# Sums of squares in DRAM, x loaded ahead for the last rows, and six places for stationary operands, in a bidirectional hybrid layer

## The chip, the cores and the metric

The kernel runs on one core of a Trainium2 chip. The core has a matrix engine (PE, with its weight loads shown apart as PEld), a vector engine (DVE), a scalar engine (ACT), GpSimd (POOL), and SyncE (SP), whose queue issues nearly all transfers. The engines run side by side; each takes its own instructions in order and waits on semaphores for the others. The metric is the device time of one execution in microseconds (us).

## The reference, cut to what matters

```python
h = rms_norm(x, norm_g) * (1 + scale) + shift          # scale, shift, gate from silu(c) @ w_ada
z = h @ w_in + b_in                                    # 2048 x 2048 times 2048 x 4096
u_pool, u_lru, g_pool, g_lru = four quarters of z
y_pool = pool_mixer(u_pool)                            # windowed means, 256 x 256 product per group
y_lru  = rg_lru(conv4(u_lru))                          # gates by products, a scan each way, summed
y_pool = rms_norm(y_pool, out_norm_pool_g) * silu(g_pool)
y_lru  = rms_norm(y_lru,  out_norm_lru_g)  * silu(g_lru)
y = concat(y_pool, y_lru) @ w_out + b_out              # 2048 x 2048 times 2048 x 2048
out = rms_norm(x + gate * y, final_norm_g)
```

Everything is float32, the sequence has 2048 rows and the model width is 2048. The two middle norms need, for each row, the sum of squares over the 1024 channels of the pooling half and over the 1024 of the recurrent half, that is over four groups of 256 channels each.

## The kernel before, in words

**Steps.** The program is one loop over 368 steps t. A step is 24 matmuls of 128x512: a stationary operand `s` (in pool `s`) against a moving operand `m` (three places, pool `m`). Both are float32 numbers split in two parts, and three of the four products of parts are taken, so a product of 128 channels costs three matmuls. Steps 0 to 255 are the input projection: eight groups of 32 steps (L0, P3, L1, L2, P2, L3, P1, P0; L is a recurrent head, P a pooling group), in each four blocks `tb` of 512 rows with eight steps. Steps 256 to 367 are the output projection, in two halves `sg` of 56 steps; each does seven products instead of eight by sums and differences of quarter matrices (A11, A12, S2, S3, A22, S1, S4), eight steps a product, first for q=0 and then for q=1.

**Lists by step.** `at(t, fn)` puts work into step t, behind its matmuls. `m_load` issues the moving operand four steps ahead, `m_split` (L160: ACT copy L169, DVE subtraction L170) splits it two steps ahead. `unit_load` and `unit_split` (L267, L285) make a stationary operand of the output projection; u counts them, four for a product, and `unit_at` says in which step. SP's queue has loads and stores in one order, and an instruction that waits there holds up those behind it.

**Gated groups.** For each group and block, `merge` (L563, recurrent) or `fin` (L637, pooling) multiplies the result with its gate and stores it to DRAM (`yscr`). It also squares it (L570, L648) and adds the squares to a tile of 128x2048 (L572, L650): `sq["L"]` and `sq["P"]`, each in one of the eight places of pool `big`. The last pooling group has its blocks at steps 240, 246, 250 and 256, the last recurrent head its blocks 3, 2, 1, 0 at 225, 231, 237 and 243.

**Norms.** `rn(tb, kind)` (by `rms_chain`, L391) takes a block's slice: one float32 matmul with a matrix of ones (L393) sums over partitions, then ACT takes the root (L394) and DVE the reciprocal (L395). The eight calls stand at steps 244 to 259. `normed` (L278) multiplies the stored groups with it when they become stationary operands; blocks 0 and 1 are used in the first half, blocks 2 and 3 in the second.

**Rows out.** `out_evac` (L712) gathers the products in row tiles `o` (eight places of `big`). For each row tile and half of its columns `x_load` brings x into a place of pool `raw` (eight places, shared by all loads), `x_add` (L744) adds `b_out` times gate (`gb`), `part_fin` (L748) multiplies with the gate, adds x, and squares on ACT (L755); `out_row` (L763) sums the squares, takes root and reciprocal, scales (L775) and stores. The last four steps (364 to 367) are held back and done tile by tile, with `part_fin` and `out_row` of each tile behind it; the moving operand of step 367 is called `ml`.

**Order.** A list scheduler at build time sets each engine's order. It takes the program's order as priority and lets an instruction pass when another isn't ready by its reckoning. PE, DVE and ACT then run that order whatever is late.

Of the kernel before, what the change touches and what calls it, by code (L numbers as in the profile page):

```python
# [44 lines left out]
def layer(ctx: ExitStack, tc: tile.TileContext, xc, xn, c, wada, win, wgate, wpool, wout, vecs, consts, bout, fng, out):  # L45
    nc = tc.nc
    pool = lambda name, bufs, **kw: ctx.enter_context(tc.tile_pool(name=name, bufs=bufs, **kw))
    one = pool("one", 1)
    s_p = pool("s", 8)
    m_p = pool("m", 3)  # L50
    raw_p = pool("raw", 8)
    big_p = pool("big", 8)

    mix_pools = [tc.alloc_tile_pool(name=n, bufs=b, side="right") for n, b in (("tmp", 9), ("gw", 1), ("uch", 1))]
    tmp_p, gw_p, uch_p = mix_pools
# [41 lines left out]
    def V(name, i, n=1):  # L97
        return vec[:, VO[name] + i:VO[name] + i + n]
# [123 lines left out]
    def c_fin():  # L222
# [3 lines left out]
            nc.tensor.matmul(out=ps[:, n:n + 1], lhsT=a[:, n * 128:(n + 1) * 128], rhs=ones[:, 0:1], start=True, stop=True)  # L226
        vtt(out=bias, in0=ps[:, 0:4], in1=V("b_in", 0, 4), op=ALU.add)

    def w_split(g, p):
        r = wraw.pop((g, p))  # L230
        s = s_p.tile([128, 2, 2, TB], F32R, tag="s", name="s")
# [243 lines left out]
        vtt(out=w[:, 1], in0=r, in1=w.bitcast(F32)[:, 0], op=ALU.subtract)  # L475
        gw["t"] = w

    def sq_alloc(kind):
        t = big("sq" + kind)[:, :S]
        nc.gpsimd.memset(t, 0.0)  # L480
        sq[kind] = t

    def lru_unit(g, h, d, tb, b, last):

# [78 lines left out]
        def merge():  # L563
            hf, gr = st["hf"], st["g"]
            silu(g, gr)
            for i in range(2):
                vtt(out=hf[:, i], in0=hf[:, i], in1=st["t", i], op=ALU.add)
            for i in range(2):
                stt(out=gr[:, i], in0=hf[:, i], scalar=V("gn_lru", 2 * h + i), in1=gr[:, i], op0=ALU.mult, op1=ALU.mult)
                act(out=hf[:, i], in_=hf[:, i], func=AF.Square)  # L570
                v = sq["L"][:, tb * TB:(tb + 1) * TB]
                vtt(out=v, in0=v, in1=hf[:, i], op=ALU.add)  # L572
            store(out=yscr[g][tb], in_=gr)
            if last:
                del u_t[g]

# [13 lines left out]
    def pool_unit(g, q, tb, b, last):  # L590
        w = WINDOWS[q]
        lo = w // 2
        hi = w - lo - 1
        st = {}

        def sums():
            if tb == 0:
                r = raw("pwr")
                load(out=r[:, :, :256], in_=wpool[q])
                pw = raw_p.tile([128, 2, 2, 256], F32R, tag="raw", name="pw")  # L600
                act(out=pw[:, 0], in_=r[:, :, :256], func=AF.Copy)
                vtt(out=pw[:, 1], in0=r[:, :, :256], in1=pw.bitcast(F32)[:, 0], op=ALU.subtract)
                gw["p"] = pw
            U = u_t[g]
            st["x"] = x = uch_p.tile([128, 2, 2, TB], F32R, tag="uch", name="uch")
            for i in range(2):
                t = tmp("pt")
                n = TB + w - 2
                o = PAD + tb * TB - lo
                eng = vtt  # L610
                eng(out=t[:, :n], in0=U[i][:, o:o + n], in1=U[i][:, o + 1:o + 1 + n], op=ALU.add)
                k = 2
                while k < w:
                    n -= k
                    eng(out=t[:, :n], in0=t[:, :n], in1=t[:, k:k + n], op=ALU.add)
                    k *= 2
                t = t[:, :TB]
                if tb == 0:
                    vtt(out=t[:, :lo], in0=t[:, :lo], in1=cst[:, EO[w]:EO[w] + lo], op=ALU.mult)
                if tb == 3 and hi:  # L620
                    vtt(out=t[:, TB - hi:], in0=t[:, TB - hi:], in1=cst[:, EO[w] + lo:EO[w] + lo + hi], op=ALU.mult)
                stt(out=t, in0=t, scalar=1.0 / w, in1=U[i][:, usl(tb)], op0=ALU.mult, op1=ALU.subtract)
                act(out=x[:, 0, i], in_=t, func=AF.Copy)
                vtt(out=x[:, 1, i], in0=t, in1=x.bitcast(F32)[:, 0, i], op=ALU.subtract)
            if last:
                del u_t[g]

        def mix():
            for m in range(2):
                ps = px()  # L630
                for j in range(2):
                    mm3(ps, gw["p"], slice(m * 128, (m + 1) * 128), st["x"], j, j == 0, j == 1)
                st["ps", m] = ps
            st["g"] = raw("gl")
            load(out=st["g"], in_=gscr[g][tb])

        def fin():  # L637
            gr = st["g"]
            for m in range(2):
                c_ = 2 * q + m  # L640
                y = tmp("py")[:, :TB]
                act(out=y, in_=st.pop(("ps", m)), func=AF.Identity, scale=V("pool_scale", c_), bias=pbias[:, c_:c_ + 1])
                st["y", m] = y
            silu(g, gr)
            for m in range(2):
                y = st["y", m]
                stt(out=gr[:, m], in0=y, scalar=V("gn_pool", 2 * q + m), in1=gr[:, m], op0=ALU.mult, op1=ALU.mult)
                act(out=y, in_=y, func=AF.Square)  # L648
                v = sq["P"][:, tb * TB:(tb + 1) * TB]
                vtt(out=v, in0=v, in1=y, op=ALU.add)  # L650
            store(out=yscr[g][tb], in_=gr)

        at(b, sums)
        at(b + 1, mix)
        at(b + 2, fin)
# [29 lines left out]
    def rows_open():  # L685

        for p in reversed(mix_pools):
            p.release()
        row_p = ctx.enter_context(tc.tile_pool(name="row", bufs=1, side="right", reuse_waits="tile"))
        for n in ("gb", "fg", "gate"):  # L690
            fin[n] = row_p.tile([128, D], F32, tag=n, name=n)
        load(out=fin["gb"], in_=bout.broadcast_to([128, D]))
        load(out=fin["fg"], in_=fng.broadcast_to([128, D]))
        fin["rn"] = row_p.tile([128, 4, TB], F32, tag="rn", name="rn")
        for i, (tb, kind) in enumerate([(2, "P"), (2, "L"), (3, "P"), (3, "L")]):
            act(out=fin["rn"][:, i], in_=rn_t[tb, kind], func=AF.Copy)
            rn_t[tb, kind] = fin["rn"][:, i]
        sq.clear()

    def gate_rows(i):  # L700
        t = raw("dg")[:, 0]
# [33 lines left out]
    def row_of(sg, n):  # L735
        return 8 * sg + n

    def x_load(sg, n, h):
        r = raw("x").rearrange("p j t -> p (j t)")
        i = row_of(sg, n)  # L740
        load(out=r, in_=xn[i * 128:(i + 1) * 128, h * 1024:(h + 1) * 1024])
        x_t[sg, n, h] = r
# [5 lines left out]
    def part_fin(sg, n, h, lo, hi, slot):  # L748
# [10 lines left out]
    def half_fin(sg, n, h):  # L759
        x_add(sg, n, h)  # L760
        part_fin(sg, n, h, 0, 1024, h)

    def out_row(sg, n, slots, parts):  # L763
        i = row_of(sg, n)
# [46 lines left out]
    at(134, gate_fin)  # L811

    L_START = {0: (47, 72), 2: (98, 123), 3: (149, 174), 5: (200, 225)}
    at(68, sq_alloc, "L")
    at(70, sq_alloc, "P")
    for g, (f, r) in L_START.items():
        h = GROUPS[g][1]
        at(f - 3, gw_load, h, 0)
# [20 lines left out]
    for sg in range(2):  # L839
        b = NT1 + SG * sg  # L840
        for n in range(4):
            step_b = (49 + 2 * n, 49 + n)[sg]
            for i, h, e in ((n, 0, b + 22 + 2 * n), (n + 4, 0, b + 41 + 2 * n), (n + 4, 1, b + step_b)):
                at(e - 2, x_load, sg, i, h)
                at(e, half_fin, sg, i, h)
            at(b + 50 + n, x_load, sg, n, 1)
            if sg == 0:
                at(b + 52 + n, x_add, sg, n, 1)
# [25 lines left out]
    for i in range(4):  # L874
# [167 lines left out]
```

## Time and profile before

| what | us |
|---|---|
| median of 3 runs | 2274.22 |
| their range | 2274.2 to 2274.82 |
| the profiled execution, its whole time | 2274.88 |
| its span, first to last instruction | 2272.7 |
| PE busy | 2241.9 |
| DVE busy | 1656.3 |
| ACT busy | 1294.4 |

The terms of a sum are read from the profiled execution and are therefore set against 2274.88, of which 2.2 lie outside the span. "Busy" is time in which an engine has an instruction running. A wait is put down to the event that came last before the engine went on.

### The profile page before, as it was taken

The page shows a single profiled execution, that of the slowest core. Times are in us where ns is not written, and L with a number is a line of the kernel's source. Part 1 is how long each engine was busy: PE and PEld are TensorE (multiplying, and loading weights), DVE is VectorE, ACT ScalarE, POOL GpSimd, SP SyncE. Part 2 cuts the span into 40 slices and gives each one's busy share as a digit, 9 for nine tenths or more (in the row PEclk, how much of TensorE's full clock was granted, in tenths as well). Part 3 has the DMA queues.
Part 4 walks back from the last instruction along what each step waited for, and adds up shares of the span by engine and source line. Part 5 has one row for each costly group of instructions (what it writes and reads, how often), then busy time and mean ns, then how long its engine had stood idle before and what let it go on. Part 6 is the DMA issues. An engine that isn't in the chain of part 4 may idle for free.

```text
span 2272.7 us, 26096 instructions
## 1 busy us (share of the span) xinstructions
PE 2241.9 (99%) x9832; PEld 1845.5 (81%) x9832; DVE 1656.3 (73%) x1986; ACT 1294.4 (57%) x1609; POOL 6.2 (0%) x40
## 2 busy tenths in 40 slices
PE   7999999999999999999999999999999999999996
PEld 6888888888888888888888888887788888888885
DVE  7999677478867564677675657668976668977579
ACT  4555677576755666666667467678643333443332
POOL 0000000000000000000000000000000000000000
PEclk9999999999999999999999999999999999999998
DMA  9878766445956654674466446654787657897555
GB/s 390 330 281 334 262 218 225 178 158 202 342 184 235 241 180 172 213 245 158 168 251 238 176 171 228 233 200 168 268 306 277 216 192 241 318 364 259 187 177 203
DMA packets 139455, 533.55 MB, mean 235 GB/s; under 512 B 15424, under 2 KB 16704, under 8 KB 131392
## 3 DMA queue, kind: packets, MB, share of 16 engines
q1 hardware_dynamic: 139328, 531.88, 65.1%
q8 instruction: 77, 1.26, 0.2%
q14 instruction: 50, 0.41, 0.1%
HBM read 417.52 MB, written 114.29 MB: 234 GB/s over the span
## 4 chain that ended last, share of the span: by engine, by line
PE 95%; DVE 3%; DMA 1%; issue 0%; ACT 0%; SPq 0%; DVEq 0%
PE pm L310 75%; PE px L310 20%; DVE o L775 1%; DMA ada<-in_wada_dram 1%; DMA xr<-in_xc_dram 0%; PE px L393 0%; DVE sqP L395 0%; DVE m L170 0%; DVE o L754 0%; DVE o L753 0%; DVE sqL L395 0%; DVE o L725 0%; PE px L707 0%; DVE x L746 0%; DVE th L549 0%
## 5 line engine op out<-in xcount | busy, mean ns | idle before, releaser
L310 PE MATMUL pm<-m,s 128*128 128x512 f32 x7674 | 1771.0, 390 | 0.0
L310 PEld LDWEIGHTS pm<-m,s 128*128 128x128 f32 x7674 | 1440.8, 188 | 304.0 <-issue 4.1
L169 ACT ACTIVATE m<-xr 128x1024 fp32r<-128x1024 f32 x366 | 386.4, 1056 | 587.0 <-PE pm L310 396.8
L170 DVE TENSOR_TENSOR m<-xr,m 128x1024 fp32r<-128x1024 f32 x366 | 446.2, 1219 | 359.8 <-ACT m L169 348.1
L310 PE MATMUL px<-m,s 128*128 128x512 f32 x1134 | 270.7, 392 | 13.8 <-ACT m L359 12.4
L310 PEld LDWEIGHTS px<-m,s 128*128 128x128 f32 x1134 | 213.6, 189 | 60.3 <-ACT m L359 12.4
L310 PE MATMUL px<-uch,gw 128*128 128x512 f32 x768 | 186.8, 391 | 0.0
L310 PEld LDWEIGHTS px<-uch,gw 128*128 128x128 f32 x768 | 144.3, 188 | 31.5 <-ACT sqL L394 0.5
L378 DVE CUSTOM_DVE_ANT_0 ada<-ada,cact 128x2048 f32<-128x2048 f32 x47 | 107.4, 2285 | 11.7 <-DMA ada<-in_wada_dram 11.7
L520 DVE TENSOR_TENSOR ig<-ig,u 128x512 f32<-128x512 f32 x64 | 44.1, 689 | 58.7 <-ACT ig L518 58.7
L303 ACT ACTIVATE s<-yr 128x1024 fp32r<-128x1024 f32 x56 | 59.0, 1053 | 46.3 <-DVE yr L299 21.8
L539 DVE SCALAR_TENSOR_TENSOR th<-rg,th 128x512 f32<-128x512 f32 x64 | 42.5, 683 | 51.7 <-ACT th L534 51.3
L304 DVE TENSOR_TENSOR s<-yr,s 128x1024 fp32r<-128x1024 f32 x56 | 68.2, 1218 | 12.3 <-ACT s L303 12.2
L235 DVE TENSOR_TENSOR s<-wr,s 128x1024 fp32r<-128x1024 f32 x56 | 68.1, 1215 | 1.0 <-ACT s L234 1.0
L185 ACT ACTIVATE xr<-xr,shv 128x512 f32<-128x512 f32 x64 | 44.3, 719 | 34.2 <-DVE xr L184 29.5
L755 ACT ACTIVATE x<-o 128x1024 f32<-128x1024 f32 (+1 forms) x36 | 34.7, 965 | 50.6 <-DVE o L754 49.1
L234 ACT ACTIVATE s<-wr 128x1024 fp32r<-128x1024 f32 x56 | 58.6, 1046 | 3.8 <-PE pm L310 2.0
L504 ACT ACTIVATE uch<-u 128x512 fp32r<-128x512 f32 x64 | 38.8, 626 | 37.3 <-DVE u L499 37.2
L253 DVE TENSOR_TENSOR tr<-tr 128x1024 f32<-128x1024 f32 x32 | 39.1, 1221 | 22.3 <-DMA tr<-in_wout_dram 21.3
L518 ACT ACT_TABLE_LOAD x42 | 53.9, 1283 | 0.7
L499 DVE SCALAR_TENSOR_TENSOR cv<-u,vec,cv 128x512 f32<-128x512 f32 x64 | 45.8, 743 | 6.7 <-ACT cv L497 6.7
L518 ACT ACTIVATE ig<-px,vec 128x512 f32<-128x512 f32 x64 | 43.7, 683 | 10.7 <-PE px L310 10.2
(161 smaller groups left out, 1658.3 us busy)
## 6 DMA issues: line engine op xcount, KB each, us to landing
xr<-xs SPq DMA_DIRECT2D x192, 512.0 KB, 5.4
ada<-in_wada_dram SPq DMA_DIRECT2D x47, 1024.0 KB, 6.9
yr<-ys SPq DMA_DIRECT2D x88, 512.0 KB, 4.7
wr<-in_win_dram SPq DMA_DIRECT2D x71, 512.0 KB, 6.0
xr<-t SPq DMA_DIRECT2D x64, 512.0 KB, 4.4
xr<-in_xc_dram SPq DMA_DIRECT2D x63, 512.0 KB, 6.3
tr<-in_wout_dram SPq DMA_DIRECT2D x48, 512.0 KB, 4.7
xr<-in_wout_dram SPq DMA_DIRECT2D x48, 512.0 KB, 4.7
```

The costliest lines, as they stand in the source:

```text
L169: act(out=m[:, 0], in_=r, func=AF.Copy)
L170: vtt(out=m[:, 1], in0=r, in1=mf[:, 0], op=ALU.subtract)
L185: act(out=r[:, j], in_=r[:, j], func=AF.Identity, bias=shv[:, k:k + 1])
L234: act(out=s[:, 0], in_=r, func=AF.Copy)
L235: vtt(out=s[:, 1], in0=r, in1=sf[:, 0], op=ALU.subtract)
L303: act(out=s[:, 0], in_=r, func=AF.Copy)
L304: vtt(out=s[:, 1], in0=r, in1=s.bitcast(F32)[:, 0], op=ALU.subtract)
L310: nc.tensor.matmul(out=ps, lhsT=a[:, x, j, asl], rhs=b[:, y, j], start=first and i == 0, stop=last and i == 2, skip_group_check=more)
L378: nc.vector.tensor_tensor_reduce(out=t, in0=t, in1=cact["t"], op0=ALU.mult, op1=ALU.add, scale=1.0, scalar=0.0, accum_out=mod[:, i:i + 1])
L499: stt(out=a if k < 3 else U[i][:, us], in0=src, scalar=cw, in1=a, op0=ALU.mult, op1=ALU.add)
L518: act(out=v, in_=st.pop(("ps", w, i)), func=AF.Sigmoid, bias=V("b_gate", (d * 4 + h) * 4 + 2 * w + i))
L520: vtt(out=st["i", i], in0=st["i", i], in1=U[i][:, us], op=ALU.mult)
```

## The change

Pool `s` has six places instead of eight, pool `big` ten instead of eight; of the eight stationary operands of an input group the last two live in `big`. The sums of squares no longer have tiles of their own. Each group and block squares both halves with one ACT instruction and sends them by a DMA from POOL's queue to a DRAM tile: a plain write the first time, an accumulating one (`accum_op=ALU.add`) for the other three groups. `rn_load` brings such a tile back a step ahead of `rn`, which now adds its two halves on DVE, does the matmul with ones, the root and the reciprocal. The four `rn` of blocks 2 and 3 move to steps 281 and 282. x for the second column half of rows 0 to 3 of each half `sg` is loaded in pairs to places of `big` at steps 29 and 31 of the half, and `x_add` follows at its steps 34 to 37; before, both stood at steps 50 to 55. The other x loads come two steps earlier, and their `x_add` one step. `unit_at` is now 250 + 2u for every u.

```diff
-    s_p = pool("s", 8)
+    s_p = pool("s", 6)
-    big_p = pool("big", 8)
+    big_p = pool("big", 10)
+    def s_tile(p):
+        return (s_p if p < 6 else big_p).tile([128, 2, 2, TB], F32R, tag="s" if p < 6 else "big", name="s")
-    def sq_alloc(kind):
-        t = big("sq" + kind)[:, :S]
-        nc.gpsimd.memset(t, 0.0)
-        sq[kind] = t
+    def sq_add(kind, tb, r):
+        if (kind, tb) in sq:
+            nc.gpsimd.dma_start(out=qscr[kind][tb], in_=r, accum_op=ALU.add)
+        else:
+            nc.gpsimd.dma_start(out=qscr[kind][tb], in_=r)
+            sq[kind, tb] = True
...
-                act(out=hf[:, i], in_=hf[:, i], func=AF.Square)
-                v = sq["L"][:, tb * TB:(tb + 1) * TB]
-                vtt(out=v, in0=v, in1=hf[:, i], op=ALU.add)
+            act(out=hf, in_=hf, func=AF.Square)
             store(out=yscr[g][tb], in_=gr)
+            sq_add("L", tb, hf)
...
+            y = raw("py")
...
-                act(out=y, in_=y, func=AF.Square)
-                v = sq["P"][:, tb * TB:(tb + 1) * TB]
-                vtt(out=v, in0=v, in1=y, op=ALU.add)
+            act(out=y, in_=y, func=AF.Square)
             store(out=yscr[g][tb], in_=gr)
+            sq_add("P", tb, y)
...
+    def x_pair(sg, n):
+        t = big("x")[:, :D].rearrange("p (i t) -> p i t", i=2)
+        i = row_of(sg, n)
+        for k in range(2):
+            load(out=t[:, k], in_=xn[(i + k) * 128:(i + k + 1) * 128, 1024:])
+            x_t[sg, n + k, 1] = t[:, k]
...
-                at(e - 2, x_load, sg, i, h)
-                at(e, half_fin, sg, i, h)
-            at(b + 50 + n, x_load, sg, n, 1)
+                at(e - 4, x_load, sg, i, h)
+                at(e - 1, x_add, sg, i, h)
+                at(e, part_fin, sg, i, h, 0, 1024, h)
+            if n % 2 == 0:
+                at(b + 29 + n, x_pair, sg, n)
+            at(b + 34 + n, x_add, sg, n, 1)
...
-                e = b + min(52 + n, 54)
-                at(e, x_add, sg, n, 1)
-                at(e, part_fin, sg, n, 1, 0, TB, 1)
+                at(b + 53 + n // 2, part_fin, sg, n, 1, 0, TB, 1)
...
-    rn_at = [(244, 1, "L"), (244, 2, "L"), (245, 3, "L"), (245, 0, "P"), (249, 1, "P"), (250, 0, "L"), (254, 2, "P"), (259, 3, "P")]
+    def rn_load(tb, kind):
+        r = raw("rq")
+        load(out=r, in_=qscr[kind][tb])
+        rn_t[tb, kind] = r
     def rn(tb, kind):
-        v = rn_t[tb, kind] = sq[kind][:, tb * TB:(tb + 1) * TB]
-        rms_chain(v, S // 2, v)
...
+        ps = px()
+        vtt(out=r[:, 0], in0=r[:, 0], in1=r[:, 1], op=ALU.add)
+        nc.tensor.matmul(out=ps, lhsT=ones, rhs=r[:, 0], start=True, stop=True)
+        act(out=v, in_=ps, func=AF.Sqrt, scale=2.0 / S, bias=epsc)
+        nc.vector.reciprocal(out=v, in_=v)
+    rn_at = [(244, 1, "L"), (246, 0, "P"), (250, 1, "P"), (251, 0, "L"), (281, 2, "P"), (281, 2, "L"), (282, 3, "P"), (282, 3, "L")]
     for t, tb, kind in rn_at:
+        at(t - 1, rn_load, tb, kind)
         at(t, rn, tb, kind)
...
-        unit_at[max(NT1 - 10 + 2 * u, NT1 - 7 + u)] = u
+        unit_at[NT1 - 6 + 2 * u] = u
```

PE's order near the end of the input projection, before, from the product of the last pooling group's block 0 (`uch,pw`) on; `gw` are the gates of the last recurrent head, `sqL` and `sqP` the matmuls with ones:

```order
L310 MATMUL px<-uch,pw 128x512 x12
L310 MATMUL pm<-m,s 128x512 x72
L393 MATMUL px<-sqL,ones 128x512 x2
L310 MATMUL px<-uch,gw 128x512 x6
...
L393 MATMUL px<-sqL,ones 128x512
L393 MATMUL px<-sqP,ones 128x512
...
L310 MATMUL px<-uch,pw 128x512 x12
L310 MATMUL pm<-m,s 128x512 x48
L393 MATMUL px<-sqP,ones 128x512
```

and the same stretch now, where `rq` is a tile of sums loaded back (of block 1 L, block 0 P, block 1 P, block 0 L in this order):

```order
L314 MATMUL px<-uch,pw 128x512 x12
L314 MATMUL pm<-m,s 128x512 x72
L878 MATMUL px<-rq,ones 128x512
L314 MATMUL px<-uch,gw 128x512 x12
...
L878 MATMUL px<-rq,ones 128x512
L314 MATMUL pm<-m,s 128x512 x24
L314 MATMUL px<-uch,pw 128x512 x12
L314 MATMUL pm<-m,s 128x512 x73
L878 MATMUL px<-rq,ones 128x512
L314 MATMUL pm<-m,s 128x512 x29
L878 MATMUL px<-rq,ones 128x512
```

The third matmul with ones now stands 73 step matmuls behind the product of block 1 from whose result its sum is finished, and the fourth 29 behind that.

SP's order in that stretch now, with the numbers of the DRAM tiles left in (`qP_215` is the sum of block 1 P, `qL_218` that of block 0 L, `ys_1_179` the gated block 1 of the last pooling group); before, no load of a sum stood here:

```order
L578 DMA ys_0_170<-gl 128x1024
L653 DMA ys_1_179<-gl 128x1024
L941 DMA ys_0_154<-yr 128x1024
L155 DMA xr<-xs_5_255 128x1024
L867 DMA rq<-qP_215 128x1024
L155 DMA xr<-xs_6_256 128x1024
L279 DMA yr<-ys_0_166 128x1024
L867 DMA rq<-qL_218 128x1024
```

The load of a sum stands behind the store of the block that completes it and ahead of loads of moving operands.

DVE's order around the last split (`ml`) before:

```order
L170 TENSOR_TENSOR m<-xr,m 128x1024
L771 RECIPROCAL rst<-rst 128x1
L754 TENSOR_TENSOR o<-o,x 128x1024
L775 SCALAR_TENSOR_TENSOR o<-o,rst,fg 128x2048
L170 TENSOR_TENSOR ml<-xr,ml 128x1024
L746 TENSOR_TENSOR x<-x,gb 128x1024
L753 TENSOR_TENSOR o<-o,gate 128x512
L769 TENSOR_TENSOR rst<-ssq 128x1
L746 TENSOR_TENSOR x<-x,gb 128x1024
```

and now:

```order
L171 TENSOR_TENSOR m<-xr,m 128x1024
L724 TENSOR_TENSOR o<-pm,o 128x512 x3
L778 SCALAR_TENSOR_TENSOR o<-o,rst,fg 128x2048
L724 TENSOR_TENSOR o<-pm,o 128x512
L171 TENSOR_TENSOR m<-xr,m 128x1024
L171 TENSOR_TENSOR ml<-xr,ml 128x1024
L760 TENSOR_TENSOR o<-o,gate 128x512 x2
L761 TENSOR_TENSOR o<-o,x 128x512 x2
L772 TENSOR_TENSOR rst<-ssq 128x1
```

Behind the last split the three adds of x (128x1024) that stood there before are gone; the last two splits stand together, with one 2048-wide scaling more ahead of them.

## Rows read from the trace of the kernel before

**Rows 1.** The page's first part: busy us (share) xinstructions.

```profile
span 2272.7 us, 26096 instructions
PE 2241.9 (99%) x9832; PEld 1845.5 (81%) x9832; DVE 1656.3 (73%) x1986; ACT 1294.4 (57%) x1609; POOL 6.2 (0%) x40
```

**Rows 2.** Waits of PE, longest first: us in total, times, longest.

```profile
PE px L310 <- ACT m L359: 12.4, 1, 12.4
PE px L310 <- DVE m L170: 0.7, 1, 0.7
```

**Rows 3.** Timeline, DVE, end: start, duration, line, operation xcount [idle before].

```profile
2222.74 1.20 DVE L746 TENSOR_TENSOR x<-x,gb 128x1024 f32<-128x1024 f32 x1
...
2235.31 1.22 DVE L170 TENSOR_TENSOR m<-xr,m 128x1024 fp32r<-128x1024 f32 x1
...
2241.04 1.22 DVE L746 TENSOR_TENSOR x<-x,gb 128x1024 f32<-128x1024 f32 x1
2242.17 0.68 DVE L753 TENSOR_TENSOR o<-o,gate 128x512 f32<-128x512 f32 x1
...
2242.85 1.22 DVE L746 TENSOR_TENSOR x<-x,gb 128x1024 f32<-128x1024 f32 x1
...
2245.25 2.35 DVE L775 SCALAR_TENSOR_TENSOR o<-o,rst,fg 128x2048 f32<-128x2048 f32 x1
2247.51 0.68 DVE L754 TENSOR_TENSOR o<-o,x 128x512 f32<-128x512 f32 x1
2248.11 1.22 DVE L746 TENSOR_TENSOR x<-x,gb 128x1024 f32<-128x1024 f32 x1
...
2258.72 0.68 DVE L725 TENSOR_TENSOR o<-pm,o 128x512 f32<-128x512 f32 x1
...
2266.21 2.74 DVE L775 SCALAR_TENSOR_TENSOR o<-o,rst,fg 128x512 f32<-128x512 f32 x4
```

**Rows 4.** Windows of the last 68 us: length, busy us of each engine, clock, DMA.

```profile
2205.00:2230.00 25.00, 25.00 (x112) 20.72 (x111) 23.23 (x25) 9.64 (x14) 0.00 (x0) 1.00 0.56 207
2230.00:2256.00 26.00, 25.28 (x109) 19.98 (x108) 25.43 (x37) 7.87 (x19) 0.00 (x0) 1.00 0.27 112
```

**Rows 5.** Timeline, PE, last matmuls.

```profile
2236.58 1.45 PE L310 MATMUL px<-m,s 128*128 128x512 f32 x5 [0.69 <-DVE m L170]
...
2254.41 1.56 PE L310 MATMUL pm<-ml,s 128*128 128x512 f32 x6
```

**Rows 6.** Timeline, PE, steps 242 to 249.

```profile
1543.50 16.50 PE L310 MATMUL pm<-m,s 128*128 128x512 f32 x72
1559.84 1.88 PE L393 MATMUL px<-sqL,ones 128*128 128x512 f32 x4
...
1588.14 11.06 PE L310 MATMUL pm<-m,s 128*128 128x512 f32 x48
```

**Rows 7.** Timeline, DVE, where two blocks are finished.

```profile
1546.31 1.40 DVE L569 SCALAR_TENSOR_TENSOR gl<-hl,vec,gl 128x512 f32<-128x512 f32 x2
...
1576.41 3.29 DVE L395 RECIPROCAL sqP<-sqP 128x512 f32<-128x512 f32 x1
...
1595.80 0.74 DVE L647 SCALAR_TENSOR_TENSOR gl<-py,vec,gl 128x512 f32<-128x512 f32 x1
```

**Rows 8.** DMA issues: KB each, median us from issue to landing.

```profile
hs<-hf SPq DMA_DIRECT2D x16, 512.0 KB, 2.9
...
gl<-gs SPq DMA_DIRECT2D x32, 512.0 KB, 5.0
...
ss<-yr SPq DMA_DIRECT2D x8, 512.0 KB, 8.0
```

**Rows 9.** Groups by line: xcount | busy us, mean ns | idle before.

```profile
L572 DVE TENSOR_TENSOR sqL<-sqL,hl 128x512 f32<-128x512 f32 x32 | 21.8, 681 | 0.0
```

**Rows 10.** Timeline, DVE: the split of stationary operand u = 35.

```profile
1982.11 1.22 DVE L304 TENSOR_TENSOR s<-yr,s 128x1024 fp32r<-128x1024 f32 x1
```

**Rows 11.** The chain that ended last: start, us, what.

```profile
1992.22 23.12 PE pm L310 x102
```

More of the change, by code (lines that the diff above doesn't have):

```diff
@@ L103, in layer @@
     tscr = [[[dram.tile([128, 2, TB], F32, name=f"t{k}_{p}_{q}") for q in range(2)] for p in range(4)] for k in range(4)]
+    qscr = {k: [dram.tile([128, 2, TB], F32, name=f"q{k}{t}") for t in range(4)] for k in "PL"}
     sscr = [dram.tile([128, 2, TB], F32, name=f"ss{p}") for p in range(4)]
@@ L227, in c_fin @@
         vtt(out=bias, in0=ps[:, 0:4], in1=V("b_in", 0, 4), op=ALU.add)
+    def s_tile(p):
+        return (s_p if p < 6 else big_p).tile([128, 2, 2, TB], F32R, tag="s" if p < 6 else "big", name="s")
     def w_split(g, p):
         r = wraw.pop((g, p))
-        s = s_p.tile([128, 2, 2, TB], F32R, tag="s", name="s")
+        s = s_tile(p)
         sf = s.bitcast(F32)
@@ L638, in fin @@
             gr = st["g"]
+            y = raw("py")
             for m in range(2):
                 c_ = 2 * q + m
-                y = tmp("py")[:, :TB]
-                act(out=y, in_=st.pop(("ps", m)), func=AF.Identity, scale=V("pool_scale", c_), bias=pbias[:, c_:c_ + 1])
-                st["y", m] = y
+                act(out=y[:, m], in_=st.pop(("ps", m)), func=AF.Identity, scale=V("pool_scale", c_), bias=pbias[:, c_:c_ + 1])
             silu(g, gr)
             for m in range(2):
-                y = st["y", m]
-                stt(out=gr[:, m], in0=y, scalar=V("gn_pool", 2 * q + m), in1=gr[:, m], op0=ALU.mult, op1=ALU.mult)
-                act(out=y, in_=y, func=AF.Square)
-                v = sq["P"][:, tb * TB:(tb + 1) * TB]
-                vtt(out=v, in0=v, in1=y, op=ALU.add)
+                stt(out=gr[:, m], in0=y[:, m], scalar=V("gn_pool", 2 * q + m), in1=gr[:, m], op0=ALU.mult, op1=ALU.mult)
+            act(out=y, in_=y, func=AF.Square)
             store(out=yscr[g][tb], in_=gr)
+            sq_add("P", tb, y)
         at(b, sums)
@@ L694, in rows_open @@
         fin["rn"] = row_p.tile([128, 4, TB], F32, tag="rn", name="rn")
[L695 to L698, printed above, removed]
     def gate_rows(i):
@@ L757, in part_fin @@
             del x_t[sg, n, h]
-    def half_fin(sg, n, h):
-        x_add(sg, n, h)
-        part_fin(sg, n, h, 0, 1024, h)
     def out_row(sg, n, slots, parts):
@@ L813, in layer @@
     L_START = {0: (47, 72), 2: (98, 123), 3: (149, 174), 5: (200, 225)}
-    at(68, sq_alloc, "L")
-    at(70, sq_alloc, "P")
     for g, (f, r) in L_START.items():
@@ L841, in layer @@
         for n in range(4):
-            step_b = (49 + 2 * n, 49 + n)[sg]
-            for i, h, e in ((n, 0, b + 22 + 2 * n), (n + 4, 0, b + 41 + 2 * n), (n + 4, 1, b + step_b)):
-                at(e - 2, x_load, sg, i, h)
-                at(e, half_fin, sg, i, h)
-            at(b + 50 + n, x_load, sg, n, 1)
+            for i, h, e in ((n, 0, b + 22 + 2 * n), (n + 4, 0, b + 41 + 2 * n), (n + 4, 1, b + (49 + 2 * n, 49 + n)[sg])):
+                at(e - 4, x_load, sg, i, h)
[4 more added lines that the diff above has]
+            at(b + 34 + n, x_add, sg, n, 1)
             if sg == 0:
-                at(b + 52 + n, x_add, sg, n, 1)
                 at(b + 56 + n, part_fin, sg, n, 1, 0, 1024, 1)
@@ L863, in start_unit @@
             pool_unit(g, GROUPS[g][1], tb, b, last)
-    rn_at = [(244, 1, "L"), (244, 2, "L"), (245, 3, "L"), (245, 0, "P"), (249, 1, "P"), (250, 0, "L"), (254, 2, "P"), (259, 3, "P")]
+    def rn_load(tb, kind):
+        r = raw("rq")
+        load(out=r, in_=qscr[kind][tb])
+        rn_t[tb, kind] = r
     def rn(tb, kind):
-        v = rn_t[tb, kind] = sq[kind][:, tb * TB:(tb + 1) * TB]
-        rms_chain(v, S // 2, v)
+        if "rn" not in fin:
+            fin["rn"] = big("rn")[:, :4 * TB].rearrange("p (i t) -> p i t", i=4)
+        r = rn_t[tb, kind]
+        v = rn_t[tb, kind] = fin["rn"][:, 2 * (tb % 2) + (kind == "L")]
+        ps = px()
[4 more added lines that the diff above has]
+    rn_at = [(244, 1, "L"), (246, 0, "P"), (250, 1, "P"), (251, 0, "L"), (281, 2, "P"), (281, 2, "L"), (282, 3, "P"), (282, 3, "L")]
     for t, tb, kind in rn_at:
+        at(t - 1, rn_load, tb, kind)
         at(t, rn, tb, kind)
```

## The prediction

> **What bounds the kernel now.** I read the page's first part first. PE is busy 2241.9 of 2272.7 us [rows 1], and the list of PE's waits holds the start (12.4 us) and nothing else above 0.7 [rows 2]. A row of the chain that ended last gives the pace: 102 matmuls in 23.12 us, 0.2267 each, so a step of 24 takes 5.44 [rows 11]. Between the start and the last matmul there is thus nearly nothing to win for a change that leaves the matmuls as they are. Each new wait of PE is paid in full.
>
> Then I read the end. The last matmul runs to 2254.41 + 1.56 = 2255.97 [rows 5], the last scaling on DVE to 2266.21 + 2.74 = 2268.95 [rows 3], and the span ends 3.75 later, with the last store. DVE, not PE, sets these 13 us: in the windows before it is busy 23.23 of 25 and 25.43 of 26 us [rows 4], and the last tile, whose matmuls end at 2255.97, is taken out only at 2258.72 [rows 3]. DVE also holds PE once, 0.69 us, by the split that starts at 2235.31 [rows 3, 5].
>
> **The end.** Of the five adds of x on DVE behind 2222, four belong to the rows whose x now comes 20 steps earlier: those at 2222.74, 2241.04, 2242.85 and 2248.11 [rows 3]. DVE starts the next instruction 1.13 after such a row starts (2241.04 to 2242.17), 0.60 after a 512-wide one (2247.51 to 2248.11), 2.26 after a 2048-wide scaling (2245.25 to 2247.51). Up to the split at 2235.31 the new order has one add of x less and two 512-wide instructions less (1.13 + 1.20), but one 1024-wide add and one scaling more (1.13 + 2.26): 1.06 more. About 1.8 us of DVE idle in the 25 of the first window [rows 4] can absorb this or not, so the split comes between 0.7 earlier and 1.1 later. I take 0.7 later, and the last matmul at about 2256.2. Behind this split DVE took 2268.95 - 2236.53 = 32.4; there go three adds (3.4), a scaling (2.26) and a 1024-wide add (1.13), and two 512-wide instructions come (1.2): 26.8, plus 0.4 for the third tile, which PE has not ready. DVE then ends at 2237.2 + 27.2 = 2264.4 to 2264.6, **4.3 earlier**. The gain can't pass 5.2: after the last matmul come three 512-wide instructions, two 1024-wide scalings, the square and the root, and four 512-wide scalings, some 7.7 us. At least it is 3.4, the three adds alone. The last store stays behind it as it is.
>
> **The sums.** On DVE 64 adds of 0.68 go (32 as in [rows 9], 32 alike for the pooling half), 43.6 us, and eight come. None lies on PE's path, so they give nothing by themselves. The eight matmuls with ones remain. But four of them now wait for a chain that did not exist: square, accumulating DMA from POOL, its landing, a load on SP, an add on DVE. Nothing in this trace accumulates in DRAM and no DMA is issued by POOL. Let A be the time from POOL's issue to landing. A plain store of the same 512 KB lands in 2.9 us and the slowest group of that size in 8.0; a load takes 5.0 [rows 8]. The accumulate must read its destination before it writes, so it should be nearer a load than a store, with a little for POOL's own part: I take 5.5, and keep 2.9 and 8.0.
>
> The Trainium skill (DMA: Bandwidth & Descriptors, section Anatomy of one DMA) fits a DMA from GpSimd by 2.0 us plus bytes over 436 GB/s, an estimate of 3.2 us for 512 KB without accumulation. No row here shows such a DMA; by it the stall worked out next would be 1.7 and the time about 2271.
>
> Block 1 L: its last product ends at 1547.71 [rows 7]; the square takes about 1.05 (two of 0.63 before), then A, a load of 5.0, an add of 0.7 and some 0.3 between engines: ready at 1554.8 + A. PE arrives after three steps at 1559.84 [rows 6], so it waits A - 5.1, or 0.4. Block 1 P: the mixing product ends at M = 1588.1, and DVE finished the block at 1596.54, M + 8.4 [rows 6, 7]. Now one reciprocal of 3.29 [rows 7] stands ahead instead of two, though it starts later: I count M + 7.3. A split's copy and the square on ACT make it M + 9.2, then A, load and add, M + 15.1 + A. PE has 73 matmuls in between, 16.55 us: it waits **A - 1.5, or 4.0**. Behind the waiting add on DVE stand splits of steps 253 and 254, behind the waiting load on SP moving operands of steps 254 to 257; both have more time than PE's wait costs, since PE stands too. Block 0 L comes 29 matmuls and the matmul with ones later, 7.7 us; root, reciprocal (0.7 + 3.3) and add ahead of it take about 6, so no wait. Block 0 P has seven steps. Sum of the stalls at A = 5.5: 4.4; at 2.9 it is 1.4, at 8.0 it is 9.4.
>
> The four late `rn` put four reciprocals in a row on DVE, 13.2 us. Two splits stand ahead of them; the third, behind, is needed 20.7 after PE has ended step 281 and is done by my count at 17.6. This costs nothing, but with 3 us less it would begin to.
>
> **Places and moved steps.** Six places suffice as long as a stationary operand is ready. The latest before, u = 35, is split at 1983.33 [rows 10]; PE needs it in step 323, which starts 78 matmuls into the row at 1992.22, at 2009.9 [rows 11]. Four steps later (21.8) leaves 4.8 us: nothing. A square holds its place in `raw` longer by about A, and pooling results now take one too; loads of moving operands wait for these on SP, but they are issued four steps, 21.8 us, ahead. The two operands in `big` take the two places that were added. I put 0.5 us of gain for the small waits around steps 244 to 252 that go, between -1 and 1.
>
> **Sum**: -4.3 - 0.5 + 4.4 = -0.4, against the profiled execution 2274.88 - 0.4 = 2274.5. The median lies 0.66 below that execution, so 2273.8.
>
> **Rivals.** First, no stall: the blocks are finished some 4 us earlier than I count, or the accumulate is as short as a store and the finish 1.5 earlier. For it speaks that DVE loses 43.6 us of adds, against it that the chain to the sum runs through scans and a reciprocal, not adds. Then only the end counts: 2274.2 - 4.8 = 2269.4, at most (5.2 + 1) 2268.0.
>
> Second, slower: the accumulating DMA takes longer than any transfer here. Both stalls grow with A, 2A - 6.6 together, and at A = 10 PE waits 13.4, less 4.8: 2282.8. It decides from A = 8.0 on, where 9.4 - 4.8 is 4.6. Against it: stores to DRAM land in 2.9 [rows 8]; for it: 8.0 occurs in the same row group for a store issued among many others, as here. The Trainium skill (same page and section) warns that a DMA's semaphore waits for the receipt of the last write, with DRAM as the slowest target; the 2.9 agrees as little as it can with a long receipt, but no row shows a read and a write in one transfer.
>
> Third, the end doesn't shrink: the last two splits slip by more than 1.1, PE waits for them and DVE's work moves behind PE. Then 2274.2 - 0.5 + 4.4 = 2278.1.
>
> **Chances.** Forecast 0.55, no stall 0.21, long accumulate 0.19, no shorter end 0.05. What a measurement can tell from no change is about 0.2%, 4.5 us: below 2269.7 or above 2278.8. The forecast with A from 2.9 to 8.0 runs from 2270.8 to 2278.8 and lies within, as does the third rival: faster 0.21, same 0.60, slower 0.19. The range 2268.6 to 2281.0 takes in nearly all of the no-stall case and the long accumulate up to A = 9.
>
> **What would show it.** The gap on PE ahead of the third L878, with the add L877 and the load of the sum as what ended it, about 4 us, and one of under 1 us ahead of the first. POOL's issue to landing of the sums, near 5.5. The last matmul to the end of DVE's scalings near 8.4 instead of 13. No L753 behind `ml`. Wrong would be: PE waits elsewhere in the middle (a late stationary operand near step 323, a split behind the four reciprocals), or 7 us and more at L878.

## The result and the profile after

The changed kernel takes **2313.98 us** (median of 4 runs, 2311.88 to 2315.54) against 2274.52 for the kernel before: ratio 1.0172, 95% interval 1.0155 to 1.019, 39.5 us slower. The prediction was 2273.8 with a range of 2268.6 to 2281.0. The profiled execution has a span of 2313.5 us where before had 2272.7 [rows 1].

The first part of the page, after (busy us, share, x instructions):

```profile
span 2313.5 us, 26084 instructions
PE 2260.5 (98%) x9832; PEld 1849.5 (80%) x9832; DVE 1623.9 (70%) x1930; ACT 1282.1 (55%) x1571; POOL 27.4 (1%) x70
```

DVE's 43.6 us of adds are gone, less new work, and PE, which set the time, is busy 18.6 us longer with the same 9832 matmuls. The other 22 us are idle time. PE's waits after (total us, times, longest):

```profile
PE px L878 <- DVE rq L877: 13.0, 2, 12.1
PE px L314 <- ACT m L363: 12.4, 1, 12.4
PE px L314 <- ACT uch L629: 5.3, 3, 3.7
PE px L314 <- ACT rg L525: 2.5, 2, 1.5
PE px L314 <- DVE uch L630: 1.7, 2, 0.8
PE px L706 <- DVE dg L703: 1.5, 1, 1.5
PE pm L314 <- ACT u L453: 1.4, 1, 1.4
PE px L314 <- ACT s L243: 1.2, 1, 1.2
```

Before, only the start (12.4) stood here above 0.7 [rows 2]. The first row is the wait that was forecast, at 12.1 + 0.9 instead of 4.0 + 0.4. The other rows, the start apart, were not forecast. They lie between steps 12 and 275 and belong to the gated groups (`uch`, `rg`), to stationary operands (`s`) and to the gate rows (`dg`).

I compared the start of each of the 368 steps in the two traces. The changed kernel is 2.0 us late at step 16, 19.2 at step 232, 27.0 at step 237, 41.2 at step 253, 44.9 at step 284 and just as late at step 360. From there to the end of the span it gains 4.1. The loss has three main parts; a smaller one, 3.5 at steps 282 and 283, is taken up with the prediction below.

**A steady drift.** Between steps 16 and 72 PE waits for nothing new and still falls behind by 0.025 us a step. Two steps of the changed kernel, one behind the other, with the sixth and the seventh stationary operand (windows: length, busy PE, PEld, DVE, ACT, POOL, clock, DMA; x counts what touches the stretch; each holds 24 matmuls):

```profile
686.76:692.20 5.44, 5.44 (x25) 4.50 (x24) 5.44 (x9) 1.06 (x1) 0.00 (x0) 1.00 0.34 114
692.20:697.80 5.60, 5.60 (x25) 4.51 (x24) 5.60 (x8) 2.33 (x3) 0.00 (x0) 1.00 0.98 349
```

The clock is 1.00 in both. The mean distance of matmuls whose operand lies in `s` is 226.8 to 227.2 ns; the seventh operand, in `big`, has 233.3 and the eighth 231.5. (In three of the eight groups the eighth operand's place has the same start address modulo 256 bytes as the places of `s`; why that matters is shown by the padded kernels below.)

**Late gates.** The largest of the unforecast waits stands at step 236. The chain behind it (start, us, what), after:

```profile
1489.20 6.13 DMA qL<-hl
...
1495.35 0.32 SPq L155
...
1495.72 7.33 DMA gs<-gr
...
1503.06 0.32 SPq L566
...
1503.43 8.12 DMA gl<-gs
...
1511.62 0.08 ACT L466
...
1524.23 0.79 PE px L314
```

The accumulating DMA reads `hl` until 1495.33 and holds its place in `raw`. The next load of a moving operand on SP (L155) wants that place. Behind it on SP stand the store of a gate (`gs<-gr`) and, at 1503, when that store has landed, the loads of the next block (L566, then `gl`). The gate lands at 1511.56, and ACT has stood at its table load for 10.54 us with the splits of `uch` queued behind. Of this the wait of L155 for the place is 3.6; the rest lies in the store, which landed after 7.33 (3.0 on the median of its row), and in the gate's load, which took 8.12 (5.1). PE then waits twice, 3.7 and 0.8 us, and starts again at half speed:

```profile
1519.00:1524.00 5.00, 0.70 (x2) 0.19 (x1) 4.69 (x9) 4.97 (x7) 0.00 (x0) 0.93 0.00 0
1524.00:1530.00 6.00, 5.76 (x14) 4.51 (x15) 5.45 (x8) 5.96 (x8) 0.00 (x0) 0.50 0.00 0
```

In the second stretch the granted clock is 0.50, the 1.2 GHz level: 14 matmuls in 6 us instead of 26, which adds about 2.6 to waits of 4.5 in sum. One row of ACT's waits sums this up, before and after:

```profile
ACT L462 <- DMA gl<-gs: 13.8, 4, 3.9
```

```profile
ACT L466 <- DMA gl<-gs: 49.3, 7, 10.5
```

**The sum of block 1 P.** Timelines of PE, SP and DVE, after (in brackets the idle time before an instruction):

```profile
1615.01 16.73 PE L314 MATMUL pm<-m,s 128*128 128x512 f32 x73
1643.88 2.08 PE L878 MATMUL px<-rq,ones 128*128 128x512 f32 x2 [12.14 <-DVE rq L877]
...
1629.86 0.85 POOL L485 DMA_DIRECT2D qP<-py  x1 [1.04 <-ACT py L652]
...
1639.96 0.32 SPq L867 DMA_DIRECT2D rq<-qP  x1
1643.13 0.69 DVE L877 TENSOR_TENSOR rq<-rq 128x512 f32<-128x512 f32 x1 [6.33 <-DMA rq<-qP]
```

The product of the block ends at 1615.0. POOL issues its squares 14.9 us later, not 9.2, and they land 10.1 later, not 5.5. From SP's issue of the load to DVE's add it took 3.2, less than the 5.0 I had counted.

**The end** after (PE's last matmuls, DVE's last scalings):

```profile
2298.39 1.56 PE L314 MATMUL pm<-ml,s 128*128 128x512 f32 x6
...
2281.16 1.22 DVE L171 TENSOR_TENSOR ml<-xr,ml 128x1024 fp32r<-128x1024 f32 x1
...
2307.25 2.74 DVE L778 SCALAR_TENSOR_TENSOR o<-o,rst,fg 128x512 f32<-128x512 f32 x4
```

DVE needs 27.6 us from the end of the last split to its end, where before needed 32.4 [rows 3]; 27.2 was forecast.

### The profile page after: what moved, and what is told of

It is laid out like the page before. It is cut to its first block, busy times and chain, and to the rows that moved or that the text cites. A ratio compares the mean times of both kernels' runs of the same rounds, so it can differ in the third digit from the quotient of the medians.

```text
span 2313.5 us, 26084 instructions
## 1 busy us (share of the span) xinstructions
PE 2260.5 (98%) x9832; PEld 1849.5 (80%) x9832; DVE 1623.9 (70%) x1930; ACT 1282.1 (55%) x1571; POOL 27.4 (1%) x70
## 5 line engine op out<-in xcount | busy, mean ns | idle before, releaser
L314 PE MATMUL px<-m,s 128*128 128x512 f32 x1134 | 270.4, 392 | 13.6 <-ACT m L363 12.4
L314 PEld LDWEIGHTS px<-m,s 128*128 128x128 f32 x1134 | 213.7, 189 | 59.8 <-ACT m L363 12.4
L284 DVE TENSOR_TENSOR yr<-yr,rn 128x512 f32<-128x512 f32 x64 | 41.6, 687 | 46.7 <-DMA yr<-ys 46.4
L238 ACT ACTIVATE s<-wr 128x1024 fp32r<-128x1024 f32 x56 | 58.7, 1049 | 14.8 <-DMA wr<-in_win_dram 14.8
L314 PE MATMUL px<-uch,pw 128*128 128x512 f32 x192 | 52.5, 417 | 7.2 <-ACT uch L629 5.3
L466 ACT ACT_TABLE_LOAD x23 | 29.5, 1283 | 53.8 <-DMA gl<-gs 49.3
```

The costliest lines, as they stand in the source:

```text
L284: vtt(out=r[:, j], in0=r[:, j], in1=rn_t[2 * sg + h, "PL"[k]], op=ALU.mult)
L314: nc.tensor.matmul(out=ps, lhsT=a[:, x, j, asl], rhs=b[:, y, j], start=first and i == 0, stop=last and i == 2, skip_group_check=more)
```

## Experiments

All times are medians on the chip; the ratio is to the kernel before, run beside it. The kernels with many waits scatter (operands in `s`: 2299.6 to 2307.8 in four executions), so by the intervals a difference between two of them is good to about 4 us. The scheduler also orders the engines anew when a kernel is edited. PE, DVE and ACT have the same order, instruction by instruction, in the changed kernel and the one with plain writes, in the kernel with three repairs and `tmp` and the one with first transfers alone, and in the kernel before and the two padded ones. In the other comparisons DVE's and ACT's orders differ in places, and what that alone costs was not measured.

| kernel | us | ratio (95%) |
|---|---|---|
| changed | 2314.0 | 1.0172 (1.0155 to 1.019) |
| operands in `s` | 2303.5 | 1.0127 (1.0114 to 1.0141) |
| squares' own place | 2297.8 | 1.0100 (1.0085 to 1.0116) |
| `rn` later | 2313.2 | 1.0167 (1.0153 to 1.0181) |
| plain writes | 2302.0 | 1.0112 (1.0097 to 1.0128) |
| three repairs | 2289.3 | 1.0058 (1.0045 to 1.0070) |
| three and `tmp` | 2281.7 | 1.0031 (1.0019 to 1.0043) |
| the same, first transfers alone | 2272.3 | 0.9991 (0.9981 to 1.0000) |
| before with the new end | 2272.1 | 0.9989 (0.9980 to 0.9997) |
| before, padded `s` | 2307.0 | 1.0140 (1.0127 to 1.0154) |
| before, `m` at 0, 64, 128 | 2305.0 | 1.0133 (1.0116 to 1.0149) |

**Operands in `s`.**

```diff
-    s_p = pool("s", 6)
+    s_p = pool("s", 8)
-    big_p = pool("big", 10)
+    big_p = pool("big", 8)
-        return (s_p if p < 6 else big_p).tile(...)
+        return s_p.tile(...)
-        t = big("x")[:, :D].rearrange(...)
+        t = s_p.tile([128, 2, 2, TB], F32R, tag="s", name="x").bitcast(F32).rearrange(...)
```

> The changed kernel, but all eight stationary operands of an input group in pool s again (eight places), pool big with eight, and the pairs of x in places of s. In the changed kernel's trace the matmuls of the operands that lie in big follow each other at 233.3 and 231.5 ns, the other six at 226.8 to 227.2; over 30 blocks of 24 matmuls each that is (6.4 + 4.6) x 720 = 7.9 us. Theory one, the place of the operand costs this: all eight operands at 226.8, the pace drift between steps 16 and 232 gone, and with the 1.4 us of the wait at step 12 for a place about 9 us less, 2305. Theory two, the slower pace comes from the traffic of the accumulating DMAs: the two operands stay slower than the six, and the time stays within 2 us of 2314.

10.5 us less, theory one. All eight operands have 226.8 to 226.9 ns, the kernel is 0.0 us late at step 72, and the wait at step 12 is gone. The DMAs of the sums were still there, so theory two falls.

**Squares' own place.**

```diff
-            act(out=hf, in_=hf, func=AF.Square)
-            sq_add("L", tb, hf)
+            s2 = sq_place()
+            act(out=s2, in_=hf, func=AF.Square)
+            sq_add("L", tb, s2)
```

(the same for `y`; `sq_place` gives the two halves of one place of `big` by turns)

> The changed kernel, but the squares are written to one place of big, in two halves by turns, and the accumulating DMA reads from there, so that the place in raw is free as soon as the square is taken. Transfers, POOL's issues and the calls of rn are the same. Theory one, the place in raw that the DMA holds blocks SP's queue behind it (loads of gates late, ACT waiting for them, then PE): the PE waits for ACT and DVE of the recurrent and pooling units between steps 80 and 240 go nearly, about 17 us with the slower clock after them, of which some is kept back by the wait at rn: 2297, range 2294 to 2301. Theory two, the 24 read-and-write transfers themselves slow the other transfers: waits and time stay, 2310 to 2315. Either way the 12.5 us wait for the sum of block 1 P stays.

16.2 us less, theory one. In the changed kernel's trace SP waits 101 us for transfers of sums, 80 of them at loads and stores of other things; the largest rows (L155 loads moving operands, L252 a weight tile, L867 the sums):

```profile
SPq L155 <- DMA qL<-hl: 25.9, 7, 6.3
SPq L867 <- DMA qP<-py: 18.4, 2, 9.8
SPq L252 <- DMA qP<-py: 14.4, 4, 6.9
SPq L155 <- DMA qP<-py: 11.6, 3, 7.4
```

With the squares' own place practically only the loads of sums are left:

```profile
SPq L878 <- DMA qP<-sqb: 11.8, 2, 7.4
SPq L878 <- DMA qL<-sqb: 2.3, 1, 2.3
```

ACT's wait for the gates falls from 49.3 to 36.3 only. It is 25.3 with three repairs and `tmp` and 11.8 when 24 transfers are left out (13.8 before), so the held places explain a part of the late gates and the transfers another.

The wait for the sum of block 1 P didn't stay as forecast but fell from 12.1 to 5.7, and one of 4.8 came for block 1 L. Block 1 P in this kernel:

```profile
1607.01 16.50 PE L314 MATMUL pm<-m,s 128*128 128x512 f32 x72
1629.19 2.08 PE L889 MATMUL px<-rq,ones 128*128 128x512 f32 x2 [5.68 <-DVE rq L888]
...
1614.47 0.85 POOL L494 DMA_DIRECT2D qP<-sqb  x1
```

The product of the block ends at 1607.0 and POOL issues the squares 7.5 us later, not 14.9; they land after 10.2 as before. So with the places in `raw` free the chain to the sum is 7 us shorter too. For block 1 L, PE arrives 10.8 us after POOL's issue in both kernels, but here the squares took 6.1 to land instead of 5.0, and from SP's issue of the load to DVE's add it took 8.7 instead of 5.8. The profiled execution is the slowest of four (2304.8, the others 2296.7 to 2298.7); it loses 4.6 us between steps 330 and 360, where the changed kernel loses nothing.

**`rn` later.**

```diff
-(250, 1, "P"), (251, 0, "L")
+(254, 0, "L"), (256, 1, "P")
```

> The changed kernel, but rn of block 0 L stands in step 254 instead of 251 and rn of block 1 P in step 256 instead of 250. Theory: the wait of 12.5 us at step 252 and the slower matmuls behind it (15.7 us in all) are nothing but the chain to the sum, and three to six more steps (16 to 33 us) cover it: 2298.5, range 2296 to 2302. Rival: the loads on SP and the add on DVE that wait for the sum hold up what stands behind them, and the stall moves to a moving operand or stationary operand: 2305 to 2314.

Theory falls: 0.8 us. The wait at `rn` went (0.8 left), and 4.0 us at a split and 4.4 at the gate rows (`dg`) came, with slower matmuls behind them: between steps 256 and 276 this kernel loses 15.3 us, the changed one 0.8. PE's waits that came, SP's between 1620 and 1690 us in this kernel, two of them, and ACT's largest:

```profile
PE px L706 <- DVE dg L703: 4.4, 1, 4.4
PE pm L314 <- DVE m L171: 4.0, 2, 3.6
...
SPq L641 <- DMA qP<-py: 5.8, 1, 5.8
SPq L279 <- DMA qL<-hl: 5.3, 1, 5.3
...
ACT s L307 <- DVE yr L284: 17.3, 3, 10.8
```

The places that the sums hold now delay `yr` for a stationary operand (L279), ACT stands 10.8 us at its split, and a moving operand's split is queued behind. So the rival was right that the stall moves; by these rows it is the held places that move it, not the loads of sums.

**Plain writes.**

```diff
-            nc.gpsimd.dma_start(out=qscr[kind][tb], in_=r, accum_op=ALU.add)
+            nc.gpsimd.dma_start(out=qscr[kind][tb], in_=r)
```

> The changed kernel with the 24 accumulating DMAs made plain writes, so that only the last group's squares are in each sum (the output differs by that). In the changed kernel's trace the eight plain writes from POOL's queue landed after 3.1 to 9.2 us, 6.6 on the mean, the accumulating ones after 5.0 to 10.4, 8.6 on the mean. Theory one, a place held by any DMA from POOL's queue is the cost, accumulating adds about 2 us of some 8.6: the waits shrink by about a fifth to a quarter, 2314 - 7 = 2307, range 2302 to 2312. Rival, accumulating is the price: without it the waits of units and rn nearly go, 2290 or less.

12 us less, more than theory one and far from the rival: about 0.3 of the loss hangs on accumulating. The medians of issue to landing fall from 7.5 and 9.1 (first two rows, changed kernel) to 5.1 and 7.9:

```profile
qL<-hl POOLq DMA_DIRECT2D x16, 512.0 KB, 7.5
qP<-py POOLq DMA_DIRECT2D x16, 512.0 KB, 9.1
```

```profile
qL<-hl POOLq DMA_DIRECT2D x16, 512.0 KB, 5.1
qP<-py POOLq DMA_DIRECT2D x16, 512.0 KB, 7.9
```

**Three repairs together**, with `rn` at (246, 0 P), (254, 0 L), (257, 1 L), (259, 1 P).

> The changed kernel with three repairs together: stationary operands and pairs of x in pool s with eight places, squares written to a place of big from which the accumulating DMA reads, and rn of block 0 L in step 254, of 1 L in 257, of 1 P in 259. All 32 transfers of sums stay. Theory: place of the operand (about 10 us), place held in raw (16 us) and the wait for the sums (14 to 16 us) are the whole loss, and the shorter end remains: 2272 as the end alone gave, plus up to 5 us for small waits at the units near steps 83, 95, 189 and 236 that were left with the squares' own place: 2275, range 2271 to 2279. Rival: the transfers of sums cost something by themselves on the queues that feed PE: 2282 or more.

24.7 us less, not 39: the number is on the rival's side. The parts one by one had given 10.5, 16.2 and 0.8. By step starts the kernel still loses 6.4 us up to step 238, then 7.2 between steps 256 and 258 and 4.8 between 272 and 276. The changed kernel loses nothing and 1.8 at the last two places, so part of what was taken away came back further on.

**Three repairs and `tmp`.**

```diff
-            y = raw("py")
+            y = [tmp("py")[:, :TB] for m in range(2)]
...
-        r = raw("rq")
-        load(out=r, in_=qscr[kind][tb])
+            r = [tmp("rq")[:, :TB] for m in range(2)]
+            for m in range(2):
+                load(out=r[m], in_=qscr[kind][tb][:, m])
```

(the loads so for blocks 0 and 1 alone)

> The kernel with the three repairs, and two users fewer of pool raw: the pooling results lie in pool tmp again, as halves, and the sums of blocks 0 and 1 are loaded into two places of tmp each (two loads of 256 KB instead of one of 512). Transfers of sums and steps of rn as with the three repairs, which took 2289.3 and whose trace still showed PE waits by late loads into raw near steps 95, 132, 189 and 236 (6.5 us in all), 257 (7.3) and 275 (4.1). Theory, what was left is places of raw as well: most of the 17 us goes, 2276, range 2272 to 2281. Rival, it is the order of SP's queue with four loads of sums and late stores among the loads of steps 246 to 275: 2284 to 2290.

7.5 us less, between the two: places of `raw` again, but not all.

**First transfers alone.**

```diff
         if (kind, tb) in sq:
-            nc.gpsimd.dma_start(out=qscr[kind][tb], in_=r, accum_op=ALU.add)
+            pass
```

> The kernel with three repairs and pool tmp for the pooling results and sums (2281.7), with the 24 accumulating DMAs left out; the eight first, plain writes and all loads of the sums stay, so the output lacks three of four groups in the two norms' sums. Theory, the transfers as such still cost what is left in the middle (2.0 us at step 132, and late loads of gates: ACT waits 25 us for them, 14 before): these waits go and the time falls by 2 to 4, 2278.5. Rival, it is the order of the loads on SP and the engines' new order, not the transfers: within 1.5 us of 2281.7. In both the 5 to 6 us near step 275 stay, where no transfer of a sum stands.

9.4 us less, and the waits near step 275 went too, against both. By the step starts of the two traces the 24 transfers cost 2.0 us at step 132, 1.5 at 257, 5.8 from 273 to 276. In the kernel with them the DMA engines' share between steps 254 and 275 is 0.87 (last but one column):

```profile
1625.00:1755.00 130.00, 125.29 (x530) 98.99 (x528) 87.86 (x101) 56.00 (x69) 0.86 (x1) 0.99 0.87 295
```

Without them the same steps have 0.82. The last two transfers there are issued at 1621.6 and 1657.1. At one load of a sum SP also waits for a transfer's landing, and that wait is gone without them:

```profile
SPq L881 <- DMA qP<-sqb: 4.3, 1, 4.3
```

So the 9.4 us hold the traffic and the waiting for its landing together. That a delay in so full a stretch is not made up until step 275 would fit too, but only the sum of the effect is shown, not its way.

**Before with the new end.** The second half of the change on the kernel before: x pairs in places of `s`, adds, x loads and `unit_at`.

> The kernel before with the second half of the change alone: x for the second column half of rows 0 to 3 in pairs (in places of pool s, which keeps eight), their adds, the other x loads and adds earlier, and the stationary operands of the output projection four steps later. Sums of squares, rn and pools as before. Theory: the end gets shorter by what it did in the changed kernel (last matmul to end of span 13.6 instead of 16.7 us), and nothing else moves: 2274.5 - 3.2 = 2271.3, range 2269.5 to 2272.5. Rival: the later stationary operands or the earlier x loads cost PE a wait, in sum no gain: 2273 to 2277.

2.4 us less (0.9989, 0.9980 to 0.9997), within the forecast range, though the interval reaches into the rival's 2273. With the sums in on-chip memory this kernel is as fast as the one above that leaves 24 transfers out. In its trace the gain behind step 360 is 3.7.

**Before, padded `s`**, to learn why `big` is slow.

```diff
+    def s_place():
+        t = s_p.tile([128, 4 * TB + 16], F32R, tag="s", name="s")
+        return t[:, :4 * TB].rearrange("p (i j t) -> p i j t", i=2, j=2)
```

> The kernel before with 64 bytes left free behind each of the eight places of pool s, so that the places start at 32, 96, 160, 224, 288, 352, 416 and 480 bytes beyond a multiple of 512 instead of all at 32 (the moving operands stay at 32); nothing else moves. In the changed kernel the operands at 32 beyond a multiple of 512 had 226.7 to 227.9 ns a matmul, those at 96, 352 and 416 had 233.0 to 233.5. Theory one, the start address sets the pace: places at 32 and 288 stay at 226.8, the others take about 233, so six of eight places x 8832 matmuls x 6.4 ns = 42 us more, 2317, range 2300 to 2325. Rival, it is the pool's neighbourhood or what else uses big at the time, not the address: all places at 226.8 and the time within 2 us of 2274.5.

32.2 us more, theory one, though 224 and 480 cost less than thought. The addresses are those that the built programs give their tiles. Four steps of 24 matmuls, with the operand at 96, 160, 224 and 288:

```profile
755.70:761.30 5.60, 5.60 (x25) 4.51 (x24) 2.65 (x3) 5.37 (x8) 0.00 (x0) 1.00 0.43 145
694.88:700.47 5.59, 5.59 (x26) 4.53 (x25) 5.59 (x9) 2.33 (x3) 0.00 (x0) 1.00 0.52 188
689.38:694.88 5.50, 5.50 (x26) 4.51 (x25) 5.50 (x8) 1.06 (x1) 0.00 (x0) 1.00 0.93 366
733.68:739.15 5.47, 5.47 (x25) 4.51 (x24) 5.47 (x9) 2.33 (x3) 0.00 (x0) 1.00 0.95 296
```

Over all steps the mean distance is 227.3 ns at 32, 233.4 at 96, 233.0 at 160, 229.1 at 224, and the same again at 288, 352, 416 and 480.

**Before, `m` at 0, 64 and 128**, `s` at 0.

> The kernel before with all places of pool s at a multiple of 256 bytes instead of 32 beyond one, and the three places of the moving operands at 0, 64 and 128 beyond a multiple of 256 instead of all at 32; nothing else moves. So far a matmul took 226.7 to 227.4 ns with the stationary operand at 32, 229.1 at 224, 232.9 at 160, 233.4 at 96, all with the moving operand at 32, and 233.5 with the stationary at 32 and the moving operand ml at 224. Theory one, only how far the two addresses lie apart counts: 226.7 at moving 0, as at 32 and 32 now, about 233 at 64 and 128 (two thirds of the steps, 8832 x 2/3 x 6.4 ns = 37.7 us): 2312, range 2290 to 2316. Theory two, each address counts by itself: steps with the moving operand at 0 take another pace than 226.7, faster or slower, and those at 64 and 128 differ from 233.

30.3 us more. Three steps, with the moving operand at 0, 128 and 64:

```profile
1942.93:1948.42 5.49, 5.49 (x26) 4.50 (x25) 5.49 (x5) 1.33 (x2) 0.00 (x0) 1.00 0.85 277
1948.42:1954.01 5.59, 5.59 (x26) 4.50 (x24) 5.43 (x7) 1.67 (x2) 0.00 (x0) 1.00 0.53 192
1954.01:1959.51 5.50, 5.50 (x25) 4.51 (x24) 5.05 (x10) 2.17 (x6) 0.00 (x0) 1.00 0.66 215
```

With `m` at 0 the second half of a step has 226.7 ns; the first half follows a slower step, and its matmuls still have up to 233.8 on the mean. So 0 against 0 is as fast as 32 against 32, as theory one says. At 64 the mean is 229.4, at 128 it is 232.9; theory one as written gave about 233 for both. It holds if the difference has a sign: stationary minus moving is -64, or 192 modulo 256, for the former, and 192 had 229.1 in the kernel with padded `s`.

## Why the prediction was wrong

**The end: right.** Forecast 4.3 earlier; it gained 4.1 behind step 360, 0.95 of them the split's stall, which I had not taken off. So the last matmul came earlier than I thought and DVE ended 10.0 behind it, not 8.4. The new end alone is worth 2.4 by medians, with an interval of 0.7 to 4.5; the 4.8 that the forecast took off for the end and the small waits lies just above it.

**Places and moved steps: this step failed first, and it cost most.** "loads of moving operands wait for these on SP, but they are issued four steps, 21.8 us, ahead" counted the slack of the loads with the longest lead, and put the extra transfers themselves at nothing. SP's queue is one: a moving operand that waits for a place holds up the gate `gl` behind it, which is loaded one or two steps ahead of its use. ACT then stops at it with everything queued behind, and PE pays twice, for the wait and for the slow clock after it. Put at nothing, the held places cost 16.2 us (squares' own place, with a chain to the sum that also got shorter). `py` and `rq` in `raw` cost 7.5 more, and the 24 transfers with the waits for their landing 9.4. The prediction had named waits elsewhere in the middle, and 7 us or more at L878, as signs of being wrong; both came.

**"The two operands in `big` take the two places that were added": 0, in truth 10.5.** I counted places and didn't ask where they lie. About 8 of it is pace, (6.4 + 4.6) ns x 24 matmuls x 30 blocks; 1.4 is the wait at step 12; the rest is within the scatter.

**The sums: mechanism right, sizes wrong.** (A is the time from POOL's issue to landing, M the end of the mixing product, as in the prediction.) Block 1 P: 12.1 us for 4.0. POOL issued at M + 14.9 instead of M + 9.2, since ACT had other blocks' work and a late `py` ahead; A was 10.1, not 5.5; load to add took 3.2, not 5.0. With 5.7 and 4.6 more and 1.8 less, the forecast's own sum gives 12.5. With the squares' own place POOL issued at M + 7.5 and A stayed 10.2: so the late issue came with the held places, and A was mis-sized by itself. Over all transfers A was 3.1 to 10.4. The Trainium skill's fit (DMA: Bandwidth & Descriptors, Anatomy of one DMA), 3.2 us by estimate, agrees with the fastest of the eight plain writes, 3.1, but not with the other seven (5.4 to 9.2) and with no accumulating one (5.0 to 10.4). Block 1 L waited 0.9 for 0.4. The prediction counted a wait at its length; with the slower matmuls behind it the one of block 1 P cost 14.8 between steps 250 and 253. With A near 10 this is the second rival's mechanism; alone it gave 2282.8, 31 short of the result.

**Stationary operands four steps later, four reciprocals in a row, x loads earlier: nothing, right.** The kernel with the new end has the first and the last and loses nothing to them. Between steps 281 and 284 the changed kernel loses 3.5, where four matmuls with ones stand now. Before they stood among steps 244 to 259: there it gains 2.6 between steps 245 and 250 and 1.6 more from 253 to 272.

**What adds up.** Changed 2314.0; three repairs 2289.3; without `py` and `rq` in `raw` 2281.7; without the 24 transfers 2272.3; the new end alone 2272.1. The loss of some 42 us against the new end is thus taken away step by step, the last 9.4 by leaving transfers out. How the 24.7 of the three repairs divides among them is not shown: together with what came back further on they are no sum of the single ones.

## What to carry to other kernels

A tile that is also a DMA's source is occupied until that DMA has landed: before a sum moves to DRAM, look who waits for its place, and on an in-order queue look at the load with the shortest lead behind that waiter, not at the waiter's own slack. When an operand of a matmul moves to another pool, keep its address relative to the other operand, or measure one step of matmuls in each place. Waits move: taking one away (`rn` later) gave 0.8 us, since others came behind it while their cause, the held places, was still there.

## What the runs showed of the hardware

The pace of these 128x512 matmuls, split float32, at full granted clock depends on the start address of the stationary operand minus that of the moving operand, modulo 256 bytes: 226.7 ns at 0, 233.4 at 64, 232.9 at 128, 229.0 to 229.4 at 192. The eleven address pairs of the two padded kernels fit it, and so does `ml` in the changed kernel (`s` at 32, `ml` at 224, difference -192 or 64: 233.4). Address differences that are not multiples of 64 were not run.
